# Delta rule on one core: doubling steps on 64 columns, sums of squares by a column of ones, and a new order between the dense products

## The chip, the core and the metric

The kernel runs on one core of a Trainium2 chip. Its engines are named as the profile names them: PE (TensorE matmul), PEld (its weight load), DVE (VectorE), ACT (ScalarE), POOL (GpSimd), SP (SyncE, which here issues the weight transfers). The metric is device time in microseconds (us); lower is better.

## The reference, cut to what matters

One decoder layer: a projection of 512 tokens by `w_in`, a gated delta rule over 8 heads, latent attention over 8 heads, an output projection and a gated feed-forward part. The change touches the delta rule of a head (and the order in which its steps stand between the products with `w_in`). With chunks of c = 64 tokens it is

```python
q = l2_normalize(q) * (dk ** -0.5)
k = l2_normalize(k)
gc = jnp.cumsum(g, axis=-1)
a_mat = jnp.where(strict, einsum("bhncd,bhnjd->bhncj", kb, k) * decay, 0.0)
sol = triangular_solve(a_mat + eye(c), concatenate([vb, kb * exp(gc)[..., None]]), lower=True)
u, w = sol[..., :dv], sol[..., dv:]
# then a scan over the chunks, with a state of 128 x 128
```

`l2_normalize` needs the sum of squares of each token's 128 channels. The triangular system is what the doubling steps solve. In the kernel a chunk is 128 tokens: NT = 4 tiles of P = 128.

## The kernel before

**Dense products.** All products with weights are made of two parts of float32r: `load_w` fetches a block of weights into `raw` (SP), ACT casts it to `whi` (L136), DVE makes the rest `wlo` (L137), and `mm3` (L143 to L145) issues three matmuls of 512 columns. One such block serves 24 matmuls. `raw` has two buffers, `whi` and `wlo` three, so a cast waits until PE is done with the block three before. Products collect in four PSUM banks `acc`.

**Delta rule.** `delta(h)` is a generator of three steps for a head. Step one transposes k (`transposed`, L466) to tokens on partitions, squares it on ACT with a running sum (L473, eight ACT instructions), takes the decays from one matmul (`gT`, L479), the products of k with k and q (`bank<-kq`), forms `bm`, and inverts the diagonal blocks of 16: `dd` (L511) goes out to DRAM and comes back replicated (`dr`, `rep`, L512 and L513, both issued by ACT's queue), and fifteen pairs of small DVE instructions (`xt`, `xs`, L519 and L521) end in `R` (L522). It also transposes v, and q only for its sum of squares (L547). Step two is `flip` (four transposes of R, L529, copied to `T` by ACT) and three doubling steps for b = 16, 32, 64: four matmuls of `bm` with `R`, a mask product on DVE (`Y`, L557), four matmuls of `T` with `Y`, and a subtraction on the odd blocks of R (L564); then the scan over the four tiles and the norm, which writes `on` in the buffer of `kbe` (L606). Step three transposes `on` (L611). These matmuls are plain float32: the trace has two PE instructions for each, and one for each transpose. They use four PSUM banks `bank`, shared by everything in `delta`.

**Order.** A string sets the order in which the steps of the heads of a pair (0 and 1) and of the dense products (p, a half of a part, 48 matmuls) are written down: `ORDER` for the first three pairs of heads, `LAST` for the fourth. The tile framework's list scheduler then places each instruction, in that order of priority, where its own planned times say it is ready, engine by engine. On the chip each engine works its list strictly in order. Heads 0, 2, 4, 6 are the even heads (the first of a pair), 1, 3, 5, 7 the odd ones.

Of the kernel before, what the change touches and what calls it, by code (L numbers as in the profile page):

```python
# [17 lines left out]
P = 128  # L18
# [15 lines left out]
# steps of a pair of heads of the delta rule (0, 1) between steps of the dense products (p)  # L34
ORDER = "0pp0p1pppp01p1"
LAST = "0pp0pp011pppppp1"
# [3 lines left out]
NEG = -1.0e30  # L40

C_UP, C_ONE, C_CAUS = (i * P for i in range(3))
C_LV = 3 * P
C_FREQ = C_LV + len(LEVELS) * P
# [8 lines left out]
def _pieces():  # L53
    """2*pi as three parts of 9 bits and a remainder."""
    out, rest = [], TWO_PI
    for k in range(3):
        e = math.floor(math.log2(rest))
        q = 2.0 ** (e - 8)
        c = math.floor(rest / q) * q
        out.append(c)  # L60
        rest -= c
    out.append(float(np.float32(rest)))
    return out
# [5 lines left out]
def _constants():  # L69
# [7 lines left out]
    for i, b in enumerate(LEVELS):  # L77
        blk = r // b
        m = (blk[:, None] % 2 == 0) & (blk[None, :] == blk[:, None] + 1)
        c[:, C_LV + i * P:C_LV + (i + 1) * P] = m  # L80
# [8 lines left out]
def layer_kernel(ctx: ExitStack, tc: tile.TileContext, x, positions, w_in, a_log, dt_bias, w_uq, w_ukv,  # L89
# [8 lines left out]
    def banks(**tags):  # L98
        """The eight banks of PSUM, by use, from here on."""
# [16 lines left out]
    def load_w(src, k, n, dst=None):  # L116
        """[P, k, n] of a weight as two float32r parts whose sum it is."""
# [45 lines left out]
    def over_tiles(ap):  # L163
        return ap.rearrange("p (o c) -> p o c", o=1).broadcast_to([P, NT, P])

    def rsq(out_ap, in_ap):
        """in ** -0.5"""
# [66 lines left out]
    def rows_of(pl_, col, dst, tag, bufs=1):  # L234
        """A scale per token, over tokens on the free side."""
# [39 lines left out]
    def split(dst_h, dst_l, src, w=None):  # L275
        """src (times a weight per partition) as two float32r parts."""
# [8 lines left out]
    def rotate(src, his, los, t1, t2):  # L285
        """Rotary of [2 x 64, tokens], each half in two parts."""
# [8 lines left out]
    def row(name, bufs=2):  # L295
        """Scratch of [P, S] in the slots of the delta rule."""
        return gd.tile([P, S], F32, name="s_" + name, tag=name, bufs=bufs)

# [34 lines left out]
    def gates():  # L333
# [9 lines left out]
        # log(1 + e) = 2 atanh(s), s = e / (2 + e) <= 1/3  # L343
# [32 lines left out]
    def rotary_tables():  # L376
        """cos and sin, frequencies on partitions."""
# [25 lines left out]
    heads = {}  # L403

    def project(hp, pre=()):
        """q, k, v (convolved, silu) and silu(z) of two heads, channels on partitions, in eight steps."""
# [43 lines left out]
    def delta(h):  # L450
        """A head of the delta rule, in three steps."""
# [17 lines left out]
        # decays between the tokens of a chunk  # L469
        ssk, rk, rk2, s1, s2, s3, ssq = (small(n) for n in ("ssk", "rk", "rk2", "s1", "s2", "s3", "ssq"))  # L470
        ktm = transposed(kT)
        for t4 in range(NT):
            nc.scalar.activation(junk, ktm[:, t4, :], AF.Square, accum_out=ssk[:, t4:t4 + 1])  # L473
        nc.vector.tensor_scalar(out=ssk, in0=ssk, scalar1=EPS, scalar2=None, op0=ALU.add)
# [11 lines left out]
        # B, of which what lies above the diagonal is never used, and the products of q and k  # L486
# [13 lines left out]
        # R = ((I + B)^-1)^T: blocks of 16 by substitution, a column of each block to a partition  # L500
        T, R, Y = sq("T", 1), sq("R"), sq("Y", 1)
# [30 lines left out]
        # k and v with tokens on partitions, scaled  # L532
# [12 lines left out]
        qtm = transposed(qT)  # L545
        for t4 in range(NT):
            nc.scalar.activation(junk, qtm[:, t4, :], AF.Square, accum_out=ssq[:, t4:t4 + 1])  # L547
# [3 lines left out]
        # and twice the size at each step  # L551
        flip(R, T)
        for i, b in enumerate(LEVELS):
            zp = bank()
            for t4 in range(NT):
                mm(zp[:, t4 * P:(t4 + 1) * P], bm[:, t4, :], R[:, t4, :])
            nc.vector.tensor_tensor(out=Y, in0=t4view(zp),  # L557
                                    in1=over_tiles(cst[:, C_LV + i * P:C_LV + (i + 1) * P]), op=ALU.mult)
            dp = bank()
            for t4 in range(NT):  # L560
                mm(dp[:, t4 * P:(t4 + 1) * P], T[:, t4, :], Y[:, t4, :])
            odd = R.rearrange("p t c -> p (t c)").rearrange("p (n w b) -> p n w b", w=2, b=b)[:, :, 1, :]
            dodd = dp.rearrange("p (n w b) -> p n w b", w=2, b=b)[:, :, 1, :]
            nc.vector.tensor_tensor(out=odd, in0=odd, in1=dodd, op=ALU.subtract)  # L564
# [3 lines left out]
        # -W^T, then the scan over the chunks  # L568
# [28 lines left out]
        # norm, gate  # L597
# [3 lines left out]
        nc.vector.tensor_scalar(out=ssq, in0=ssq, scalar1=EPS, scalar2=EPS * P, op0=ALU.add, op1=ALU.mult)  # L601
        nc.vector.scalar_tensor_tensor(out=sso, in0=sso, scalar=1.0 / P, in1=ssq, op0=ALU.mult, op1=ALU.add)
        rsq(f, sso)
        on = sq("kbe", 1)
# [10 lines left out]
    def latent(c0, accs):  # L615
        """A latent before its norm, channels on partitions, in four steps."""
# [15 lines left out]
    def normed(accs, w4, h_, l_, direct):  # L632
        """A latent, normalised, in two parts."""
# [32 lines left out]
    def dense():  # L666
        """The products with w_in, a step at a time."""
# [12 lines left out]
    # for the even head of a pair [low; high] parts, for the odd head [high; low]  # L680
# [315 lines left out]
```

## Time and profile before

| | us |
|---|---|
| median of 3 runs | 2462.61 (2461.74 to 2462.67) |
| span of the profiled execution | 2460.5 |
| PE busy in it | 2398.0 (97%) |
| PEld busy | 1965.9 (80%) |
| DVE busy | 1149.4 (47%) |
| ACT busy | 707.8 (29%) |

The span runs from the first to the last instruction; the runs' time is some 2 us longer. PE's busy time is a union of modelled matmul durations that overlap, so the distance from one start to the next, not the duration, is what a matmul costs in a row of them. The delta rule lies between 100 and 680 us of the span. In front of it and behind it PE works on products with weights.

### The profile page before, as it was taken

To read this page: it belongs to the slowest core of one execution; us is meant where nothing else is said; L and a number is where in the kernel's file an instruction comes from. 1 tells how busy PE (TensorE), PEld (TensorE's weight loads), DVE (VectorE), ACT (ScalarE), POOL (GpSimd) and SP (SyncE) were. 2 spreads that over 40 slices of the span, in tenths; PEclk is the share of its full clock that TensorE was granted. 3 is DMA by queue.
4 is the path that set the end of the run, shared out by engine and by line. 5 is a ranking of instruction groups with operands and counts; after the bars stand their busy time and mean duration, and the time that the engine had idled before them with its cause. 6 is when DMAs were issued, how large, how long until landed. Compare 5 with 4: busy or idle time off the path is not lost.

```text
span 2460.5 us, 27597 instructions
## 1 busy us (share of the span) xinstructions
PE 2398.0 (97%) x11142; PEld 1965.9 (80%) x11142; DVE 1149.4 (47%) x1850; ACT 707.8 (29%) x1154; POOL 80.1 (3%) x89
## 2 busy tenths in 40 slices
PE   8989999999999999999999999999999999999998
PEld 6777787777777778888888888888888888888886
DVE  6656565655555555433434333333334343434245
ACT  5332323333233333422222222222222222222223
POOL 0010101010000000000000000000000000000000
PEclk9999999999999999999999999999999999999999
DMA  5313232222422322333233333233333333332333
GB/s 177 79 52 78 69 87 62 85 69 70 133 69 65 90 65 67 106 95 102 86 103 97 101 94 99 89 103 94 104 94 95 102 95 95 102 95 87 107 98 111
DMA packets 199663, 225.87 MB, mean 92 GB/s; under 512 B 17264, under 2 KB 161776, under 8 KB 199408
## 3 DMA queue, kind: packets, MB, share of 16 engines
q1 hardware_dynamic: 194608, 214.15, 28.9%
q10 hardware_dynamic: 4928, 9.97, 1.3%
q8 instruction: 87, 1.43, 0.2%
q14 instruction: 40, 0.33, 0.0%
HBM read 219.63 MB, written 4.46 MB: 91 GB/s over the span
## 4 chain that ended last, share of the span: by engine, by line
PE 79%; DVE 3%; DMA 2%; ACT 2%; issue 1%; POOL 1%; ACTq 0%; POOLq 0%; DVEq 0%
PE acc L143 18%; PE acc L144 18%; PE acc L145 18%; PE bank L144 6%; PE bank L145 6%; PE bank L143 6%; PE bank L148 2%; PE score L148 1%; DMA rep<-dr 1%; DMA raw<-in_w_down 1%; PE op L148 1%; DVE wlo L137 1%; DVE t L290 0%; ACT whi L136 0%; PE bank L799 0%
## 5 line engine op out<-in xcount | busy, mean ns | idle before, releaser
L137 DVE TENSOR_TENSOR wlo<-raw,whi 128x1024 fp32r<-128x1024 f32 x386 | 469.1, 1215 | 714.5 <-ACT whi L136 708.4
L136 ACT CAST whi<-raw 128x1024 fp32r<-128x1024 f32 x386 | 403.7, 1046 | 1230.6 <-PE acc L144 687.2
L144 PE MATMUL acc<-fl,whi 128*128 128x512 f32 x1408 | 547.8, 389 | 0.0
L145 PE MATMUL acc<-fh,wlo 128*128 128x512 f32 x1408 | 547.7, 389 | 0.0
L143 PE MATMUL acc<-fh,whi 128*128 128x512 f32 x1408 | 547.6, 389 | 0.0
L144 PEld LDWEIGHTS acc<-fl,whi 128*128 128x128 f32 x1408 | 264.3, 188 | 54.9
L145 PEld LDWEIGHTS acc<-fh,wlo 128*128 128x128 f32 x1408 | 264.3, 188 | 54.8
L143 PEld LDWEIGHTS acc<-fh,whi 128*128 128x128 f32 x1408 | 264.2, 188 | 54.8
L143 PE MATMUL acc<-hh,whi 128*128 128x512 f32 (+1 forms) x656 | 266.6, 406 | 1.7 <-ACT whi L136 1.7
L144 PE MATMUL acc<-hl,whi 128*128 128x512 f32 (+1 forms) x656 | 265.6, 405 | 0.0
L145 PE MATMUL acc<-hh,wlo 128*128 128x512 f32 (+1 forms) x656 | 264.9, 404 | 0.0
L143 PE MATMUL bank<-whi,ah 128*128 128x512 f32 x640 | 249.0, 389 | 0.0
L144 PE MATMUL bank<-wlo,ah 128*128 128x512 f32 x640 | 249.0, 389 | 0.0
L145 PE MATMUL bank<-whi,al 128*128 128x512 f32 x640 | 249.0, 389 | 0.0
L918 DVE SCALAR_TENSOR_TENSOR x<-bank,rstd,x 128x512 f32<-128x512 f32 x160 | 119.8, 750 | 151.6 <-PE bank L145 151.6
L143 PEld LDWEIGHTS acc<-hh,whi 128*128 128x128 f32 (+1 forms) x656 | 124.5, 190 | 28.0 <-ACT whi L136 2.1
L144 PEld LDWEIGHTS acc<-hl,whi 128*128 128x128 f32 (+1 forms) x656 | 124.9, 190 | 26.0
L145 PEld LDWEIGHTS acc<-hh,wlo 128*128 128x128 f32 (+1 forms) x656 | 124.4, 190 | 26.2 <-issue 0.2
L143 PEld LDWEIGHTS bank<-whi,ah 128*128 128x128 f32 x640 | 120.1, 188 | 25.0
L145 PEld LDWEIGHTS bank<-whi,al 128*128 128x128 f32 x640 | 120.1, 188 | 24.9
L144 PEld LDWEIGHTS bank<-wlo,ah 128*128 128x128 f32 x640 | 120.1, 188 | 24.9
L143 PE MATMUL acc<-whi,mgh 128*128 128x512 f32 x256 | 103.4, 404 | 2.8 <-ACT mgh L278 2.5
(282 smaller groups left out, 2258.9 us busy)
## 6 DMA issues: line engine op xcount, KB each, us to landing
raw<-in_w_gate SPq DMA_DIRECT2D x88, 512.0 KB, 3.6
raw<-in_w_up SPq DMA_DIRECT2D x88, 512.0 KB, 3.6
raw<-in_w_down SPq DMA_DIRECT2D x88, 512.0 KB, 3.8
raw<-in_w_in SPq DMA_DIRECT2D x80, 512.0 KB, 3.7
raw<-in_w_out SPq DMA_DIRECT2D x32, 512.0 KB, 4.0
rep<-dr ACTq DMA_DIRECT2D x8, 512.0 KB
x<-in_x ACTq DMA_DIRECT2D x4, 1024.0 KB, 8.3
raw<-in_w_ukv SPq DMA_DIRECT2D x32, 128.0 KB, 2.6
```

The lines of the kernel that those rows point to most:

```text
L136: nc.scalar.copy(hi[:, :k * n], raw[:, :k * n])
L137: nc.vector.tensor_tensor(out=lo[:, :k * n], in0=raw[:, :k * n], in1=hi[:, :k * n].bitcast(F32), op=ALU.subtract)
L143: nc.tensor.matmul(ps, lhsT=lh, rhs=rh, start=start, stop=False)
L144: nc.tensor.matmul(ps, lhsT=lh, rhs=rl, start=False, stop=False)
L145: nc.tensor.matmul(ps, lhsT=ll, rhs=rh, start=False, stop=stop)
L148: nc.tensor.matmul(ps, lhsT=l, rhs=r, start=start, stop=stop)
L918: nc.vector.scalar_tensor_tensor(out=x2[:, t4, cs], in0=a, scalar=rstd[:, t4:t4 + 1], in1=x2[:, t4, cs], op0=ALU.mult, op1=ALU.add)
```

## The change

Five edits in `delta`, and the two strings (6).

1. The sums of squares of k and q: ACT squares the whole [128 x 512] once into the buffer `T`, and four matmuls with one column of ones sum over the channels. The transposes of q and the sixteen ACT instructions with a running sum go.
2. The doubling steps multiply only the 64 columns of a tile that change (the odd blocks): the moving side of the eight matmuls of a step has 64 columns in place of 128, DVE's mask product and the masks have 256 columns in place of 512.
3. `T` is taken at the start of a head (one buffer, as before).
4. `on` is written into `es`, which has two buffers, in place of `kbe`, which has one.
5. `ssq` is scaled in one DVE instruction as it is read from PSUM.
6. `ORDER` and `LAST` put three p ahead of the second step of the even head, and take one p from behind.

Comments are left out of the new file, so its line numbers differ by some ten.

```diff
-ORDER = "0pp0p1pppp01p1"
-LAST = "0pp0pp011pppppp1"
+ORDER = "0ppp0p1ppp01p1"
+LAST = "0ppp0pp011ppppp1"
...
-        c[:, C_LV + i * P:C_LV + (i + 1) * P] = m
+        c[:, C_LV + i * HALF:C_LV + (i + 1) * HALF] = m[:, blk % 2 == 1]
...
+        T = sq("T", 1)
+
+        def squares(src):
+            s2_ = T.rearrange("p t c -> p (t c)")
+            nc.scalar.activation(s2_, src, AF.Square)
+            qp = bank()
+            for t4 in range(NT):
+                mm(qp[:, t4:t4 + 1], s2_[:, t4 * P:(t4 + 1) * P], ones[:, 0:1])
+            return qp[:, 0:NT]
+
+        nc.vector.tensor_scalar(out=ssk, in0=squares(kT), scalar1=EPS, scalar2=None, op0=ALU.add)
         ktm = transposed(kT)
-        for t4 in range(NT):
-            nc.scalar.activation(junk, ktm[:, t4, :], AF.Square, accum_out=ssk[:, t4:t4 + 1])
-        nc.vector.tensor_scalar(out=ssk, in0=ssk, scalar1=EPS, scalar2=None, op0=ALU.add)
...
-        qtm = transposed(qT)
-        for t4 in range(NT):
-            nc.scalar.activation(junk, qtm[:, t4, :], AF.Square, accum_out=ssq[:, t4:t4 + 1])
+        nc.vector.tensor_scalar(out=ssq, in0=squares(qT), scalar1=EPS, scalar2=EPS * P, op0=ALU.add, op1=ALU.mult)
...
         for i, b in enumerate(LEVELS):
+            odd = R.rearrange("p t (n w b) -> p t n w b", w=2, b=b)[:, :, :, 1, :]
             zp = bank()
             for t4 in range(NT):
-                mm(zp[:, t4 * P:(t4 + 1) * P], bm[:, t4, :], R[:, t4, :])
+                mm(zp[:, t4 * HALF:(t4 + 1) * HALF], bm[:, t4, :], odd[:, t4])
...
             for t4 in range(NT):
-                mm(dp[:, t4 * P:(t4 + 1) * P], T[:, t4, :], Y[:, t4, :])
+                hs = slice(t4 * HALF, (t4 + 1) * HALF)
+                mm(dp[:, hs], T[:, t4, :], yh[:, hs])
...
-        on = sq("kbe", 1)
+        on = es
```

What the new strings make of the lists is seen at three places. All three are of head 2; heads 4 and 6 read alike.

PE at the flip of head 2, before (`R_1919` is that head's R, `bm_1900` its B; `acc_2231` is the first product of the next pair of heads, here seven matmuls into its first block of weights, `whi_2234`):

```order
L145 MATMUL acc_2231<-hh_76,wlo_2235 128x512
L143 MATMUL acc_2231<-hh_76,whi_2234 128x512
L529 MATMUL bank_2118<-fst_68,R_1919 128x128 x4
L148 MATMUL bank_2124<-R_1919,bm_1900 128x128 x4
L144 MATMUL acc_2231<-hl_77,whi_2234 128x512
```

The same place in the changed kernel (`R_1917`, `bm_1899`; `acc_2116` and `acc_2117` are the same products as `acc_2231` and `acc_2232` before):

```order
L145 MATMUL acc_2117<-hl_77,whi_2149 128x512
L146 MATMUL acc_2117<-hh_76,wlo_2150 128x512
L539 MATMUL bank_2178<-fst_68,R_1917 128x128 x4
L149 MATMUL bank_2184<-R_1917,bm_1899 128x64 x4
L144 MATMUL acc_2116<-hh_76,whi_2288 128x512
```

The flip now stands behind two whole blocks of the next pair (`whi_2119` and `whi_2149`), 48 matmuls, and not behind seven. Between the end of the kq products and the flip there are now 135 product matmuls; there were 98 (and one between the kq products).

PE in step one of head 2, some products behind the transposes of v, before (`acc_1990` and `acc_1991` are z of this pair):

```order
L144 MATMUL acc_1991<-hl_77,whi_1993 128x512
L145 MATMUL acc_1991<-hh_76,wlo_1994 128x512
L466 MATMUL bank_1979<-fst_68,kq_1217 128x128 x4
L143 MATMUL acc_1990<-hh_76,whi_2023 128x512
L144 MATMUL acc_1990<-hl_77,whi_2023 128x512
```

And changed (`T_1881` holds the squares of q, `cst_67` the ones):

```order
L146 MATMUL acc_1987<-hh_76,wlo_1990 128x512
L144 MATMUL acc_1986<-hh_76,whi_2019 128x512
L149 MATMUL bank_1978<-cst_67,T_1881 128x1 x4
L145 MATMUL acc_1986<-hl_77,whi_2019 128x512
L146 MATMUL acc_1986<-hh_76,wlo_2020 128x512
```

Four matmuls of one column stand where four transposes stood. A second group of four stands ahead of the transposes of k, where nothing stood.

ACT around the issue of `dr` of head 2, before (`whi_2083` is the last block of z, `whi_2234` the first of the next pair):

```order
L444 ACTIVATE vt_1869<-y_1862 128x512
L136 CAST whi_2083<-raw_2082 128x1024
L547 ACTIVATE junk_1877,ssq_1884<-bank_1979 128x128 x4
L542 ACTIVATE kdec_1966<-bank_1885,sc_302 128x128 x2
L512 DMA dr_1922<-dd_1921 128x64
L542 ACTIVATE kdec_1966<-bank_1885,sc_302 128x128 x2
L513 DMA rep_1923<-dr_1922 128x1x1024
L136 CAST whi_2234<-raw_2233 128x1024
```

And changed (`whi_2079` is the last block of z, `whi_2119` and `whi_2149` the first two of the next pair):

```order
L445 ACTIVATE vt_1865<-y_1858 128x512
L493 ACT_TABLE_LOAD
L493 ACTIVATE es_1898<-es_1898 128x512
L552 ACTIVATE kdec_1964<-bank_1889,sc_302 128x128 x4
L137 CAST whi_2079<-raw_2078 128x1024
L137 CAST whi_2119<-raw_2118 128x1024
L522 DMA dr_1920<-dd_1919 128x64
L523 DMA rep_1921<-dr_1920 128x1x1024
L137 CAST whi_2149<-raw_2148 128x1024
```

The issue of `dr` now stands behind the cast of the next pair's first block, which stood behind it.

## Rows read from the trace of the kernel before

**Rows 1.** The page, busy time, share and count of each engine.

```profile
PE 2398.0 (97%) x11142; PEld 1965.9 (80%) x11142; DVE 1149.4 (47%) x1850; ACT 707.8 (29%) x1154; POOL 80.1 (3%) x89
```

**Rows 2.** Windows: stretch, us, busy and (count) by engine; clock, DMA share, GB/s.

```profile
100.00:680.00 580.00, 542.20 (x2745) 440.86 (x2744) 344.15 (x785) 197.11 (x423) 56.90 (x59) 0.98 0.28 78
1000.00:2400.00 1400.00, 1400.00 (x6197) 1159.53 (x6196) 522.84 (x565) 330.73 (x363) 1.01 (x1) 1.00 0.32 97
```

**Rows 3.** Waits of PE, 100 to 680 us: us in total, times, longest.

```profile
PE bank L529 <- DVE R L522: 18.6, 5, 4.9
PE bank L148 <- ACT kdec L542: 3.5, 1, 3.5
PE bank L466 <- DVE es L497: 3.4, 3, 1.5
...
PE bank L611 <- DVE kbe L606: 2.2, 3, 0.8
...
PE bank L466 <- DVE kbe L606: 1.5, 1, 1.5
```

**Rows 4.** Timeline: start us, us, instruction xcount, [idle before]. Waits before flip or doubling.

```profile
116.84 1.99 PE L148 MATMUL bank<-kq 128*128 128x256 f32 x8
144.56 1.09 PE L529 MATMUL bank<-fst,R 128*128 128x128 f32 x4 [4.87 <-DVE R L522]
217.08 2.05 PE L148 MATMUL bank<-Y,T 128*128 128x128 f32 x8 [3.45 <-ACT kdec L542]
243.03 1.13 PE L148 MATMUL bank<-kq 128*128 128x256 f32 x4
272.27 1.09 PE L529 MATMUL bank<-fst,R 128*128 128x128 f32 x4 [3.36 <-DVE R L522]
597.75 0.66 PE L529 MATMUL bank<-fst,R 128*128 128x128 f32 x4 [2.51 <-DVE R L522]
```

**Rows 5.** Windows, columns as in rows 2: from PE's restart to full clock.

```profile
217.08:220.31 3.23, 3.23 (x12) 2.83 (x13) 1.41 (x2) 0.00 (x0) 0.00 (x0) 0.50 0.64 195
272.27:278.34 6.07, 6.07 (x25) 5.68 (x26) 1.68 (x2) 0.59 (x1) 1.09 (x1) 0.50 0.29 86
403.76:408.04 4.28, 4.28 (x20) 3.89 (x21) 1.67 (x2) 0.59 (x1) 1.07 (x1) 0.60 0.42 123
534.31:537.76 3.45, 3.45 (x15) 3.25 (x16) 1.62 (x2) 0.59 (x1) 1.09 (x1) 0.51 0.34 92
597.76:602.60 4.84, 4.84 (x25) 4.47 (x26) 3.15 (x4) 2.26 (x3) 0.00 (x0) 0.65 0.01 3
```

**Rows 6.** Timeline of PE at full clock: a group of small matmuls, and what follows.

```profile
112.29 0.60 PE L148 MATMUL bank<-sc,cst 128*128 128x32 f32 x4 [1.71 <-DVE sc L354]
112.73 0.47 PE L144 MATMUL acc<-hl,whi 128*128 128x512 f32 x1
...
119.81 0.65 PE L466 MATMUL bank<-fst,vt 128*128 128x128 f32 x4 [0.51 <-ACT qe L485]
120.22 0.48 PE L145 MATMUL acc<-hh,wlo 128*128 128x512 f32 x1
...
152.75 1.13 PE L148 MATMUL bank<-Y,T 128*128 128x128 f32 x8
153.64 0.48 PE L143 MATMUL acc<-hh,whi 128*128 128x512 f32 x1
```

**Rows 7.** Groups by shape, 100 to 680 us: busy, mean ns, idle before.

```profile
L557 DVE TENSOR_TENSOR Y<-bank,cst 128x512 f32<-128x512 f32 x24 | 16.6, 691 | 34.5 <-PE bank L148 34.5
...
L564 DVE TENSOR_TENSOR R<-R,bank 128x256 f32<-128x256 f32 x24 | 10.1, 420 | 27.4 <-PE bank L148 27.4
```

**Rows 8.** Timeline of head 2: the inversion of the blocks on ACT and DVE.

```profile
252.91 0.32 ACTq L512 DMA_DIRECT2D dr<-dd  x1
...
255.93 1.05 ACT L136 CAST whi<-raw 128x1024 fp32r<-128x1024 f32 x1 [2.03 <-PE acc L144]
...
271.07 1.05 DVE L522 TENSOR_TENSOR R<-xs,cst 128x512 f32<-128x512 f32 x1
```

## Prediction of the time after the change

> **What bounds the kernel now.** I read the page's busy times first: PE is busy for 97% of the span, no other engine for half of it [rows 1]. Behind 1000 us PE never stops and issues a matmul every 1400 / 6197 = 0.226 us [rows 2]; the change does not reach there. In the delta rule's stretch, 100 to 680 us, PE is busy for 542.2 of 580 us at a mean clock of 0.98 [rows 2]: it is still the engine that sets the end, but 38 us of it are waits. So an edit counts in two ways only: by what it adds to or takes from PE's own list, and by what it does to those waits. DVE (344 us) and ACT (197 us) have room in the stretch, and matter as links of a chain that PE waits for.
>
> The waits of PE come next [rows 3]. Five waits at the flip, for R, make 18.6 us. They are those of head 0 (4.87), head 2 (3.36), head 7 (2.51) [rows 4] and, by subtraction, 7.9 us of heads 4 and 6 together. One wait of 3.45 us stands in the first doubling step of head 1: its matmuls of T with Y need a bank that ACT's `kdec` frees, `kdec` of that head comes behind `kbe`, and `kbe` is written only when the `on` of head 0, in the same buffer, has been transposed. The rest, 3.4 + 2.2 + 1.5 us, are short waits where a head begins [rows 3]. Behind each of the long waits PE's granted clock is at its lower level, 1.2 GHz (0.50 of full), until it is back at 2.4 GHz [rows 5]. A stretch of length w at mean clock m, in which PE never waits, costs (1 - m) x w: 3.23 x 0.50 + 6.07 x 0.50 + 4.28 x 0.40 + 3.45 x 0.49 = 1.6 + 3.0 + 1.7 + 1.7 = 8.0 us for heads 1, 2, 4 and 6.
>
> **The order: what it takes from the waits.** In head 2 the chain from the kq products to R runs from 243.03 [rows 4] to 271.07 + 1.05 = 272.12 us [rows 8], 29.1 us. PE had work for 25.9 us of that. With 135 in place of 99 product matmuls between, it has 36 x 0.226 = 8.1 us more, and 0.5 us by the squares (below): 34.5 us. But the chain grows too. `dr` is issued at 252.91; in the new list of ACT it stands behind a cast that before began at 255.93, when PE was done with an older block, and took 1.05 us [rows 8]. That makes 257.0, and 0.5 us more since PE comes 0.5 us later to that point: the chain is 4.6 us longer, 33.7 us. PE arrives 0.8 us behind R, so the waits of heads 2, 4 and 6 go: 3.36 + 7.9 = 11.3 us, with the half clock behind them. What is late next is the flip itself, by 0.8 us only; the second rival is about that.
>
> The odd heads lose products there (139 or 140 in place of 171 in heads 3 and 5) and still have 139 x 0.226 + some 3.5 us of small matmuls = 34.9 us against the 29.1 us of head 2's chain, the nearest row. No wait comes there. Head 0 has 92 in place of 82 products: 2.3 us, and 0.5 us of squares; against that I set 0.5 us, since its `rep` is now issued behind a silu of z on ACT. Its wait shrinks by 2.3 us, from 4.87 to 2.6; that is near the 2.51 us of head 7, which had half clock behind it too [rows 4, 5], so I take nothing off for the clock. Head 7 has 93 in place of 94 products: no change.
>
> **`on` in `es`** frees `kbe` of the next head at once: `kbe` and `kdec` of an odd head no longer wait for the transposes of `on`. The 3.45 us of head 1 go, with 1.6 us of clock (in the 8.0).
>
> **The 64 columns: nothing on PE.** A doubling step has 16 PE instructions. A group of eight with 128 moving columns takes 153.64 - 152.75 = 0.89 us, 0.111 each; a group of four with 32 moving columns takes 112.73 - 112.29 = 0.44 us, 0.110 each [rows 6]. Both load 128 columns of weights for every instruction. A float32 matmul with fewer moving columns is thus no cheaper, whatever holds it at 0.11 us; 64 lies between 32 and 128, and I price it at 0.111. The bounds are 0.055 (half, which is the first rival) and 0.111. On DVE the mask product falls from 0.69 to about 0.42 us, that of the 256 columns beside it [rows 7], 24 times: 6.5 us. PE covers it with product matmuls, four of 0.226 before and three in the new list: 0.90 - 0.69 = 0.21 us to spare before, 0.68 - 0.42 = 0.26 now. So nothing comes of it on PE; without that cover it would be up to 6.5 us either way.
>
> **The column of ones: a loss on PE.** Four matmuls are eight PE instructions, 8 x 0.111 = 0.89 us by the same two rows, also with one moving column. A head has two such groups and loses one group of four transposes, 120.22 - 119.81 = 0.41 us [rows 6]: 1.78 - 0.41 = 1.37 us a head, 11.0 us for eight. The bounds are 0 (one column free, less 3.3 us of transposes: a gain) and 11.0. Of ACT sixteen instructions and their reads go, two of some 0.6 us come; ACT is not what PE waits for there. The new group at the head's front waits for a square of k in `T`, which is free once the head before has done its last doubling step, long ago in PE's list. The single scaling of `ssq` is one DVE instruction of four columns less: nothing.
>
> **Banks.** Each sum takes a fifth bank at the head's front, where four exist. PE waits in order, with the dense products behind it. The short waits there (7.1 us) can grow or go: between -7 and +8 us. I take 0, since the new list has five products between the decays and the kq products and eight behind the transposes of v, where banks are freed.
>
> **The sum**, on the profiled execution: 2460.5 - 11.3 (flips of heads 2, 4, 6) - 3.45 (head 1) - 8.0 (clock) - 2.3 (head 0) + 11.0 (squares) = 2446.5 us. The runs' median is 2.1 us above the span: 2448.6, say 2449.
>
> **Rival 1, columns count.** If a float32 matmul is paid by its moving columns, the doubling steps lose 24 x 16 x 0.055 = 21 us, and the squares cost nothing and save 3.3 us of transposes: 2462.6 - 25.0 - 21 - 3.3 = 2413. For it: eight instructions of 256 columns (the kq products) last 1.99 us, eight of 128 last 1.13 [rows 4, 6]. Against it: the row of 32 columns, which is one group only. The Trainium skill, "TensorE: Matmul & The Clock Gate", section "Back-to-back issue gap", tabulates the distance by moving columns alone, 134 cycles for 128 and about 60 for 64 or fewer, which would halve these matmuls. The row of 32 columns disagrees with that for float32 with a weight load each.
>
> **Rival 2, the flips still wait.** The margin of 0.8 us in heads 2, 4 and 6 rests on one cast and on DVE's order, where the reads of the z products stand among the small instructions of the inversion. If the chain is 4 us longer than I think, the three waits come back as they were: 11.3 us and 6.4 us of clock, 2449 + 17.7 = 2466, no change that can be told.
>
> **Rival 3, slower: the fifth bank.** The sum of squares of q needs a bank that in the odd heads only the products of `es` free, behind an exponential on ACT; in the even heads that exponential now stands behind a silu and one more table load. If PE must wait there, everything dense behind it waits too. It decides from where the waits exceed 14 us in all, 1.75 us in each of eight heads; the longest such wait so far is 1.5 us, three of them make 3.4 [rows 3]. At 2.5 us each, with 1.7 us of half clock behind, it is 8 x 4.2 = 34 us: 2449 + 34 = 2483.
>
> **How the numbers follow.** Forecast 0.72 (2441 to 2457), rival 1 0.06, rival 2 0.14 (partly come back: 2455 to 2467), rival 3 0.08. The range reaches from 2438 to 2462: it takes in the short waits' bounds and the half of rival 2, and leaves out rivals 1 and 3. What a measurement can tell from no change is 0.2%, 5 us: faster is below 2457.7, slower above 2467.5. Faster is the forecast, rival 1 and a little of rival 2: 0.80; same most of rival 2 and some of rival 3: 0.14; slower 0.06.
>
> **What would show it.** In the profile of the changed kernel: PE's count in the delta rule's stretch up by 8 x (16 - 4) = 96, and by some 11 us of start-to-start time; groups of 64 columns at 0.89 us to the next start, as those of 128; groups of one column the same. No wait at the flip in heads 1 to 6, one of 2 to 3 us in heads 0 and 7, no wait for `kdec`, and granted clock below 1.00 behind heads 0 and 7 alone. Wrong would be: groups of 64 columns at half the time (rival 1), waits for R in heads 2, 4 and 6 with `rep` issued late (rival 2), or new waits at the matmuls of one column or the transposes of v (rival 3).

## The result and the profile after

| | before | changed |
|---|---|---|
| median of 4 runs, us | 2462.64 (2461.74 to 2464.68) | 2436.18 (2435.13 to 2440.96) |
| span of the profiled execution, us | 2460.5 | 2434.6 |
| first score matmul of the attention, us | 690.70 | 666.13 |

The ratio is 0.9896, with a 95% interval of 0.9884 to 0.9907: 26.4 us faster. The forecast was 2449 (13.6 us faster) with a range of 2438 to 2462. The sign was right, the size was half of what came, and the time lies 2 us below the range. Of the 25.9 us between the two spans, 24.6 lie in front of the first score matmul, as expected of a change in the delta rule. The other 1.3 us are about what a stretch at the lower clock near the end cost the kernel before (0.24 x 7.00 = 1.7 us, below), which this execution of the changed kernel did not have there.

The page of the changed kernel (as [rows 1]), its window of the delta rule (as the first of [rows 2]) and its waits of PE from 100 to 680 us (as [rows 3]):

```profile
PE 2396.4 (98%) x11238; PEld 1971.7 (81%) x11238; DVE 1137.7 (47%) x1850; ACT 704.0 (29%) x1049; POOL 79.9 (3%) x89
```

```profile
100.00:680.00 580.00, 565.08 (x2965) 466.37 (x2963) 347.94 (x808) 201.08 (x332) 59.26 (x60) 0.99 0.29 82
```

```profile
PE bank L539 <- DVE R L532: 5.4, 2, 3.5
PE acc L144 <- ACT mgh L279: 2.5, 1, 2.5
PE bank L623 <- DVE es L618: 2.3, 3, 0.8
PE bank L149 <- DVE sc L355: 1.7, 1, 1.7
```

PE has 96 instructions more, and is busy for 565.1 of the 580 us, where it was for 542.2. The waits for `R` fell from five of 18.6 us [rows 3] to two of 5.4; the wait for `kdec` is gone; and so are all short waits of the transposes at a head's front (L466 before, 3.4 + 1.5 us in [rows 3] and two of 0.6 and 0.5 that are not shown there, 6.0 in all). Of the 7.1 us that the prediction called short waits, the 2.2 us of the transposes of `on` stay (2.3 now); 4.9 us went, and 1.1 us that it had not listed. What is left by name is the two flips, the transposes of `on`, and waits that have to do with other parts.

The timeline of PE at the places of [rows 4]: the flips of heads 0, 2 and 7.

```profile
145.85 0.63 PE L539 MATMUL bank<-fst,R 128*128 128x128 f32 x4 [1.85 <-DVE R L532]
234.72 1.89 PE L149 MATMUL bank<-kq 128*128 128x256 f32 x8
269.14 0.60 PE L539 MATMUL bank<-fst,R 128*128 128x128 f32 x4
582.77 1.08 PE L539 MATMUL bank<-fst,R 128*128 128x128 f32 x4 [3.53 <-DVE R L532]
```

The flip of head 2 stands without a wait in brackets; those of heads 4 and 6 too (only two waits are left in the sum above). In head 4 it is close: R is ready 0.17 us ahead of the flip, and flips that do wait start 0.15 us behind R. Head 0 waits 1.85 us where it waited 4.87, head 7 3.53 where it waited 2.51.

Prices on PE, from one start to the next as in [rows 6]: eight instructions of one column, and eight of 64 columns, each with the row behind.

```profile
122.73 0.95 PE L149 MATMUL bank<-cst,T 128*128 128x1 f32 x8
123.54 0.48 PE L146 MATMUL acc<-hh,wlo 128*128 128x512 f32 x1
...
149.59 0.60 PE L539 MATMUL bank<-fst,R 128*128 128x128 f32 x4
150.03 1.00 PE L149 MATMUL bank<-R,bm 128*128 128x64 f32 x8
150.84 0.47 PE L146 MATMUL acc<-hh,wlo 128*128 128x512 f32 x1
...
151.38 0.40 PE L145 MATMUL acc<-hl,whi 128*128 128x512 f32 x1
151.64 1.08 PE L149 MATMUL bank<-Y,T 128*128 128x64 f32 x8
152.53 0.47 PE L146 MATMUL acc<-hh,wlo 128*128 128x512 f32 x1
...
153.31 0.60 PE L539 MATMUL bank<-fst,R 128*128 128x128 f32 x4
```

One column: 0.81 us for eight. 64 columns: 0.81 and 0.89 us for eight, and 0.89 is what 128 columns took in [rows 6]. So fewer moving columns than 128 buy nothing here; what all these instructions share is a load of 128 columns of weights. That the load is what holds them is not shown: no run has a load of fewer columns. The Trainium skill, "TensorE: Matmul & The Clock Gate", section "LDWEIGHTS (loading the stationary operand)", gives a weight load as its columns over 1.2, in ns: that makes an estimate of 107 ns for 128 columns, and the trace's 0.10 to 0.11 us agree with it; the table by moving columns that the prediction weighed does not hold for these matmuls.

The clock, by windows as in [rows 5]. First the changed kernel: behind the wait for `sc` in front of head 0, behind the flip of head 0, behind that of head 7, and behind the wait for `mgh`:

```profile
114.85:118.26 3.41, 3.41 (x11) 2.83 (x10) 3.21 (x9) 1.00 (x3) 1.03 (x1) 0.50 0.16 31
145.85:152.00 6.15, 6.15 (x45) 5.30 (x45) 2.25 (x4) 1.17 (x2) 1.08 (x1) 1.00 0.30 85
582.77:590.00 7.23, 7.23 (x32) 6.65 (x32) 1.95 (x3) 1.63 (x2) 0.00 (x0) 0.55 0.00 0
637.22:642.70 5.48, 5.48 (x20) 3.92 (x20) 3.41 (x7) 2.00 (x4) 0.64 (x1) 0.70 1.05 383
```

and the kernel before at three of the same places (flip of head 0, `sc`, `mgh`), and near its end:

```profile
144.56:150.00 5.44, 5.44 (x26) 5.07 (x27) 0.84 (x2) 1.59 (x2) 0.15 (x1) 0.63 0.07 23
112.29:118.00 5.71, 5.68 (x29) 4.35 (x30) 2.78 (x9) 3.12 (x13) 1.03 (x1) 1.00 0.24 61
662.16:667.00 4.84, 3.77 (x18) 2.71 (x19) 3.41 (x7) 2.00 (x4) 0.00 (x1) 1.00 1.04 377
2415.00:2422.00 7.00, 6.89 (x24) 5.05 (x23) 4.89 (x9) 2.00 (x5) 0.55 (x1) 0.76 0.00 0
```

The half clock behind heads 1, 2, 4, 6 and 0 is gone, but two stretches at 1.2 GHz came behind waits of 1.7 and 2.5 us that had full clock behind them before. In all (1 - m) x w is 8.0 [rows 5] + 2.0 + 1.7 (heads 0 and 7) = 11.7 us before, and 1.7 + 3.3 + 1.6 = 6.6 us after.

### The profile page after: what moved, and what is told of

The parts are those of the page before. It is cut to its first block, busy times and chain, and to the rows that moved or that the text cites. A ratio compares the mean times of both kernels' runs of the same rounds, so it can differ in the third digit from the quotient of the medians.

```text
span 2434.6 us, 27687 instructions
## 1 busy us (share of the span) xinstructions
PE 2396.4 (98%) x11238; PEld 1971.7 (81%) x11238; DVE 1137.7 (47%) x1850; ACT 704.0 (29%) x1049; POOL 79.9 (3%) x89
## 3 DMA queue, kind: packets, MB, share of 16 engines
q1 hardware_dynamic: 194608, 214.05, 29.2%
## 4 chain that ended last, share of the span: by engine, by line
PE 92%; DVE 3%; DMA 2%; ACT 1%; issue 1%; POOL 1%; ACTq 0%; SPq 0%; POOLq 0%
PE acc L144 22%; PE acc L145 22%; PE acc L146 22%; PE bank L145 6%; PE bank L146 6%; PE bank L144 6%; PE bank L149 5%; PE score L149 1%; DMA raw<-in_w_down 1%; PE op L149 1%; DVE wlo L138 1%; DMA rep<-dr 1%; ACT whi L137 0%; PE bank L539 0%; DVE t L291 0%
## 5 line engine op out<-in xcount | busy, mean ns | idle before, releaser
L144 PEld LDWEIGHTS acc<-hh,whi 128*128 128x128 f32 (+1 forms) x656 | 124.3, 189 | 29.2 <-ACT whi L137 2.1
L145 PEld LDWEIGHTS acc<-hl,whi 128*128 128x128 f32 (+1 forms) x656 | 124.3, 189 | 26.6 <-issue 0.7
```

Of the source, the lines that this page charges most:

```text
L144: nc.tensor.matmul(ps, lhsT=lh, rhs=rh, start=start, stop=False)
L145: nc.tensor.matmul(ps, lhsT=lh, rhs=rl, start=False, stop=False)
```

## The experiments: one edit alone, and all but one

There are four edits that may stand alone: the strings, the squares, the columns, and `on` in `es`. Each was made alone on the kernel before, and each was taken back alone from the changed kernel. Ratios are to the kernel before on the same chip. "Waits for R" and "head fronts" (waits of the transposes of k, q and v and of the matmuls of one column) are sums from each profile, in us; "score" is the start of the first score matmul. The last three columns are of one execution each; that of all but `on` was the slowest of its four (2439.70), and lost 3.4 us more to the lower clock than that of the changed kernel (10.2 against 6.8, from 100 us to the first score matmul).

| kernel | median, us | ratio, 95% interval | waits for R | head fronts | score |
|---|---|---|---|---|---|
| strings alone | 2447.42 | 0.9939 (0.9922 to 0.9955) | 9.5 | 5.5 | 673.9 |
| squares alone | 2468.55 | 1.0020 (1.0011 to 1.0029) | 18.1 | 3.5 | 697.9 |
| columns alone | 2467.64 | 1.0014 (1.0005 to 1.0023) | 19.6 | 3.1 | 690.3 |
| `on` alone | 2461.10 | 0.9990 (0.9981 to 0.9999) | 18.3 | 6.0 | 690.5 |
| all but the strings | 2462.96 | 1.0006 (0.9997 to 1.0015) | 17.0 | 1.1 | 691.3 |
| all but the squares | 2437.95 | 0.9905 (0.9889 to 0.9922) | 7.8 | 2.4 | 668.0 |
| all but the columns | 2442.54 | 0.9924 (0.9910 to 0.9939) | 5.1 | 0.9 | 670.1 |
| all but `on` | 2435.83 | 0.9901 (0.9886 to 0.9916) | 5.4 | 0 | 669.0 |
| changed, again | 2438.71 | 0.9906 (0.9893 to 0.9920) | 5.5 | 0 | 666.8 |

**The strings alone.**

```diff
-ORDER = "0pp0p1pppp01p1"
-LAST = "0pp0pp011pppppp1"
+ORDER = "0ppp0p1ppp01p1"
+LAST = "0ppp0pp011ppppp1"
```

> The kernel before with the two new strings alone. Theory A (the order takes the waits at the flips of heads 2, 4 and 6, and nothing else): 11.3 us of waits and 6.4 us of half clock go, head 0's wait shrinks by about 1 us, head 1's wait for kdec (3.45 us and 1.6 us of clock) and the short waits at the heads' fronts (7.1 us) stay: 2462.6 - 18.7 = 2444 us. Rival B (the order also takes the short waits at the fronts, since the dense products of a half part more lie there): 2437 us, with no squares to pay for.

They gave 16.4 us (2463.86 to 2447.42), near theory A's 2444. The waits of PE in that profile:

```profile
PE bank L529 <- DVE R L522: 9.5, 4, 4.5
PE bank L466 <- DVE vb L544: 4.9, 3, 1.7
PE bank L148 <- DVE Y L557: 2.5, 4, 0.7
```

The even heads' waits are gone, and so is the one for `kdec`, which the prediction had put down to `on` in `es`. But the short waits stay, now as 4.9 us in front of the transposes of q in the odd heads, head 7 waits 4.5 us, and small waits for `Y` are new.

**The squares alone**.

```diff
...
+        T = sq("T", 1)
...
+        def squares(src):
+            s2_ = T.rearrange("p t c -> p (t c)")
+            nc.scalar.activation(s2_, src, AF.Square)
+            qp = bank()
+            for t4 in range(NT):
+                mm(qp[:, t4:t4 + 1], s2_[:, t4 * P:(t4 + 1) * P], ones[:, 0:1])
+            return qp[:, 0:NT]
...
-        qtm = transposed(qT)
-        for t4 in range(NT):
-            nc.scalar.activation(junk, qtm[:, t4, :], AF.Square, accum_out=ssq[:, t4:t4 + 1])
+        nc.vector.tensor_scalar(out=ssq, in0=squares(qT), scalar1=EPS, scalar2=EPS * P, op0=ALU.add, op1=ALU.mult)
```

> The kernel before with the sums of squares by a column of ones alone (old strings, 128 columns, on in kbe). The list then has 111 products in place of 98 between the kq products and the flip of heads 2, 4, 6. Theory A (the transposes of q held a bank until ACT had summed its squares, and that made the short waits at the fronts): PE pays 9.2 us more, the fronts' 6 us go, and 13 products and 0.5 us shorten each of the three flip waits by 3.4 us, so 10 us and most of their 6.4 us of clock go: 2462.6 + 9.2 - 6 - 10 - 5 = 2451 us. Rival B (the fronts' waits are not the transposes of q): 2457 us.

Both missed: it is slower by 4.7 us. In the old order the flips wait as before or longer (heads 2 and 4 in its timeline; head 4 waited 3.71 before):

```profile
271.37 1.08 PE L538 MATMUL bank<-fst,R 128*128 128x128 f32 x4 [4.05 <-DVE R L531]
...
408.95 1.08 PE L538 MATMUL bank<-fst,R 128*128 128x128 f32 x4 [5.38 <-DVE R L531]
```

So what the edit takes from the short waits does not pay for its matmuls, and the flips take no part of their price: R comes later too. From the start of the kq products to the end of R it takes 33.8 us in head 2 here, and 29.1 before.

**The columns alone** and **`on` alone**:

```diff
...
-                mm(zp[:, t4 * P:(t4 + 1) * P], bm[:, t4, :], R[:, t4, :])
+                mm(zp[:, t4 * HALF:(t4 + 1) * HALF], bm[:, t4, :], odd[:, t4])
...
-                mm(dp[:, t4 * P:(t4 + 1) * P], T[:, t4, :], Y[:, t4, :])
+                mm(dp[:, hs], T[:, t4, :], yh[:, hs])
...
```

> The kernel before with the doubling steps on 64 columns alone. Theory A (a float32 matmul with 64 moving columns costs 0.111 us like one with 128, DVE's shorter mask product is covered): 2462.6 us, within 3 us. Rival (the steps get shorter all the same, by DVE's 0.27 us in each of 24 steps): 2456 us.

```diff
-        on = sq("kbe", 1)
+        on = es
```

> The kernel before with on written into es alone. Theory A (only head 1's wait for kdec goes, 3.45 us and 1.6 us of clock; the other waits stay): 2457.5 us. Rival B (kbe, freed early, also takes the short waits at the fronts of the odd heads, some 5 us): 2452 us.

`on` alone gives 0.1%, at the edge of what can be told, and not the 5 us of its theory. The columns alone come out slower by 3.8 us, and the clock accounts for that: nine of their ten runs had a mean granted clock of 0.988 or 0.989, where the 25 runs of the kernel before had 0.991 to 0.994, and 0.003 of 2466 us is 7 us. (The profiled execution was the tenth, the fastest with 2460.95 and a clock of 0.992, so its rows are some 7 us better than the median.) The long wait of head 1 did not go with `on`: PE now waits at the same place for the next link of the chain, `Y`. The waits at the first doubling step of head 1, columns alone and `on` alone:

```profile
215.85 1.08 PE L149 MATMUL bank<-Y,T 128*128 128x64 f32 x8 [2.20 <-DVE Y L560]
```

```profile
216.99 1.13 PE L148 MATMUL bank<-Y,T 128*128 128x128 f32 x8 [1.84 <-DVE Y L557]
```

Added up, the four edits alone give -16.4 + 4.7 + 3.8 - 2.8 = -10.7 us. Together they give -26.4. Nearly half of the difference is clock. By the mean granted clock m of each run of length w (on record to 0.001), (1 - m) x w is on average 18.7 us before, 11.0 with the strings, 19.7 with the squares, 26.6 with the columns, 17.0 with `on`, and 11.0 in the changed kernel: -0.5 us for the single edits added up, -7.7 for all of them together. So about 7 of the 15.7 us are clock; that is an estimate, since it also counts what falls into waits. The next four runs look for the rest by taking one edit back from the changed kernel.

**All but the strings** (old `ORDER` and `LAST` in the changed kernel).

> The changed kernel with the old strings (squares by ones, 64 columns and on in es stay). Theory A, the three edits and the order lean on each other: with the old order the flips of heads 2, 4 and 6 wait again as in the run of the squares alone (4.05, 5.38 and 4.36 us, half clock behind each), and the 9.2 us of the squares' matmuls are paid: 2464 us. Rival B, the edits add up as they did one at a time (+4.7 squares, +3.8 columns, -2.8 on, on 2463.9): 2469.5. If the order is worth only what it gave alone (-16.4), it comes to 2452.6.

Theory A: 2462.96, no change against before (1.0006). The waits for R are back, 17.0 us in five. So the strings are worth 27 us where the other edits stand (by the two ratios, 1.0006 against 0.9896), and 16 alone; and the other edits are worth nothing without the strings. What they save on PE in the old order (the fronts and `kdec`) is about what the squares' matmuls cost, and the flips of heads 2, 4 and 6 go on waiting. The chains to R, further below, show why.

**All but the squares** (squares as before in the changed kernel).

> The changed kernel with the sums of squares as before (transposes of q, sixteen ACT instructions). Theory A, the squares' edit takes the waits at the front of the odd heads away because the transposes of q, which wait there for a bank that DVE reads, are gone: PE gets back 9.2 us of matmuls, and the waits of the run of the strings alone return (three of 1.65 us in front of the transposes of q, head 0 by 2 us, flips of odd heads and first products of Y by 3 us, head 7 by 1 us, each with some 0.17 us of restart): 2436.2 - 9.2 + 12 = 2439 us. Rival B, those waits go by another edit (on in es or the columns): 2427 to 2429 us.

Theory A, 2439 expected, 2437.95 measured. Its waits:

```profile
PE bank L530 <- DVE R L523: 7.8, 3, 3.9
...
PE bank L467 <- DVE es L498: 1.9, 3, 0.7
```

The waits in front of the transposes of q return, though smaller than with the strings alone, and the flips of heads 0 and 1 wait longer. The matmuls of one column cost about 10 us of PE, and are paid back in waits: with them or without them the time is the same within the intervals.

**All but the columns** (128 columns in the changed kernel).

> The changed kernel with the doubling steps on 128 columns, as before. Theory A, columns cost nothing on PE (0.112 us for 64 and 128) and DVE's longer mask product lies beside product matmuls: 2436 us, at most 2 off. Rival B, the shorter mask products (24 times 0.27 us) shorten the waits of PE between the matmuls of a step: 2442 us. Rival C, the 64 columns cost as they seemed to alone (+3.8): 2432 us.

Rival B: 2442.54, 6 us above the changed kernel (and 6.7 above the run without `on`, on the same chip; the four runs of one and of the other do not overlap). PE's price is the same; the difference is a wait too short for the sums of waits. This is the doubling step with 128 columns, from its timeline, which answers to the rows of 64 columns above:

```profile
148.24 0.64 PE L538 MATMUL bank<-fst,R 128*128 128x128 f32 x4
148.71 1.06 PE L148 MATMUL bank<-R,bm 128*128 128x128 f32 x8
...
150.30 0.39 PE L143 MATMUL acc<-hh,whi 128*128 128x512 f32 x1
150.64 1.13 PE L148 MATMUL bank<-Y,T 128*128 128x128 f32 x8
...
152.31 0.63 PE L538 MATMUL bank<-fst,R 128*128 128x128 f32 x4
```

From the last product to the matmul with `Y` it is 0.34 us here, and 151.64 - 151.38 = 0.26 with 64 columns, where a product takes 0.23. Both have their mask product on DVE beside the products:

```profile
L564 DVE TENSOR_TENSOR Y<-bank,cst 128x512 f32<-128x512 f32 x24 | 16.5, 689 | 30.0 <-PE bank L148 30.0
```

```profile
L568 DVE TENSOR_TENSOR Y<-bank,cst 128x256 f32<-128x256 f32 x24 | 10.1, 423 | 28.4 <-PE bank L149 28.4
```

From one flip to the next a step takes 152.31 - 148.24 = 4.07 us with seven products here, and 153.31 - 149.59 = 3.72 us with six in the changed kernel. Less the products at 0.2265 us each, that is 2.48 against 2.36: 0.12 us in each of 24 steps, 3 us. Three waits at heads' fronts add 0.9, one in head 1 adds 0.6, and four more waits cost some 0.16 us more each than their rows say (the account of the prediction has why): 5.1 us. By the start of the first score matmul the two profiled executions are 4.0 us apart; this one lost 1.7 us less to the lower clock on the way (5.1 against 6.8). Without that it is 5.7 us, near the 6 us between the medians.

**All but `on`** (`on` in `kbe` in the changed kernel).

> The changed kernel with on in kbe, as before. Theory A, the prediction's step: on in es is what took head 1's wait for kdec away; it comes back with its half clock: 2436.2 + 3.5 + 1.6 = 2441 us. Rival B, the new order has taken that wait away by itself (the run of the strings alone shows no wait for kdec): 2436 us, no wait for kdec in the profile.

Rival B: 2435.83, no `kdec` among the waits. With the new order `on` in `es` does nothing that can be told.

## The experiments: which half of the squares, and a faster kernel

These four ran on one chip, the changed kernel among them (2438.71, the table's last row).

**Squares of k as before, those of q by ones.**

```diff
-        nc.vector.tensor_scalar(out=ssk, in0=squares(kT), scalar1=EPS, scalar2=None, op0=ALU.add)
         ktm = transposed(kT)
+        for t4 in range(NT):
+            nc.scalar.activation(junk, ktm[:, t4, :], AF.Square, accum_out=ssk[:, t4:t4 + 1])
+        nc.vector.tensor_scalar(out=ssk, in0=ssk, scalar1=EPS, scalar2=None, op0=ALU.add)
```

> The changed kernel with the squares of k as before (ACT, from the transposed k) and those of q by the column of ones. Theory A, the two halves of the edit do different things: the matmuls for k (64 PE instructions, 64 x 0.099 = 6.4 us) buy a shorter chain to R, those for q take the transposes of q out of the odd heads' front. So PE gains 6.4 us and loses what the flips' waits of heads 0, 1 and 7 were longer with all squares as before (3.27, 0.54, 3.95 against 1.85, 0, 3.53 us, with 0.5 us of restart and clock); no wait at a transpose of q: 2436.2 - 6.4 + 3.0 = 2433 us. Rival B, the waits of R do not come back: 2430. Rival C, what is gained on PE is lost again wholly: 2436.

All three missed: 2442.69, slower by 4.0 us than the changed kernel (their runs overlap by 0.4 us, 2441.68 to 2443.61 against 2436.73 to 2442.08), with 64 PE instructions fewer. Its waits:

```profile
PE bank L541 <- DVE R L534: 9.4, 5, 3.3
...
PE bank L149 <- DVE es L509: 1.9, 3, 0.7
```

Heads 1, 3 and 5 wait for R now, and the matmuls of one column of q wait where the transposes of q did. The head-3 flip of the changed kernel shows why that was near: R is ready at 327.82 + 1.08 = 328.90, and PE comes at 330.87.

```profile
327.82 1.08 DVE L532 TENSOR_TENSOR R<-xs,cst 128x512 f32<-128x512 f32 x1
...
330.87 0.60 PE L539 MATMUL bank<-fst,R 128*128 128x128 f32 x4
```

So it is the squares of k that keep the chain to R short in the odd heads, and not the missing transposes of q that clear the head's front. The waits that came (3.9 us for R, 2.4 at the fronts) are about the 6.4 us saved. The 4 us more are in the two traces too: 0.9 us of waits of the kq products, 11 waits more, each some 0.16 us longer than its row (1.8 us), and 1.7 us more lost to the lower clock up to the first score matmul (8.5 against 6.8).

The even heads go the other way, and there the traces show how the edits lean on each other. Two times decide at each flip: when R is ready, and when PE comes to the flip. Both are counted here from the start of the head's kq products, in us, from the timelines; head 2 stands for the even heads 2, 4 and 6, head 3 for the odd heads 3 and 5.

| kernel | head 2: R ready | PE comes | head 3: R ready | PE comes |
|---|---|---|---|---|
| before | 29.1 | 29.2 (waits) | 31.2 | 49.9 |
| strings alone | 29.6 | 35.2 | 39.4 | 39.5 (waits) |
| squares alone | 33.8 | 33.9 (waits) | 33.9 | 48.1 |
| all but the strings | 32.5 | 32.7 (waits) | 33.4 | 45.7 |
| all but the squares | 29.6 | 35.3 | 37.5 | 38.1 |
| squares of k as before | 32.4 | 35.7 | 39.6 | 39.6 (waits) |
| changed | 33.6 | 34.4 | 33.8 | 35.8 |

With the strings alone PE comes 6 us later to the even heads' flips and 10 us earlier to the odd ones, where R also comes 8 us later (what holds it there stays open). That leaves 5.6 us to spare in the even heads and none in the odd ones. There a shorter chain counts, and the other edits shorten it: the columns and `on` from 39.4 to 37.5 us, the squares to 33.8. In the old order R has 12 us and more to spare in head 3, so the same edits gain nothing there. The squares also make R 4 us later in the even heads (29.1 to 33.8 with the old strings, 29.6 to 33.6 with the new): in the old order the flips wait for that, in the new one it falls into the room that the strings made. Of k alone, with the new strings, R is 1.2 us later in head 2 and 5.8 earlier in head 3.

These are the rows of `dr` and R of head 2, with the strings alone (its kq products start at 236.99):

```profile
246.89 0.32 ACTq L512 DMA_DIRECT2D dr<-dd  x1
...
265.49 1.08 DVE L522 TENSOR_TENSOR R<-xs,cst 128x512 f32<-128x512 f32 x1
```

and with the squares alone (from 237.46):

```profile
250.97 0.32 ACTq L521 DMA_DIRECT2D dr<-dd  x1
...
270.17 1.05 DVE L531 TENSOR_TENSOR R<-xs,cst 128x512 f32<-128x512 f32 x1
```

The new place of `dr` on ACT, behind two casts, was shown ahead of the prediction as the work of the new strings, and the prediction priced it there. It is the squares': with the strings alone `dr` goes out 9.9 us behind the kq products and ahead of the second cast, as before; with the squares alone it goes out after 13.5 us, behind two casts, as in the changed kernel. This is read from the traces and not tested by itself: each edit makes the scheduler write all lists anew, and no run changes an edit and keeps the lists, so what a run shows is the edit with its lists.

**Squares and ones in float32r**, two columns of ones:

```diff
+    onr = const.tile([P, 2], F32R, name="onr")
+    nc.vector.tensor_copy(onr, ones[:, 0:2])
...
-        T = sq("T", 1)
+        s2_ = gd.tile([P, S], F32R, name="sqr", tag="T", bufs=1)
...
-                mm(qp[:, t4:t4 + 1], s2_[:, t4 * P:(t4 + 1) * P], ones[:, 0:1])
-            return qp[:, 0:NT]
+                mm(qp[:, 2 * t4:2 * t4 + 2], s2_[:, t4 * P:(t4 + 1) * P], onr[:, 0:2])
+            return qp[:, 0:2 * NT:2]
...
+        T = sq("T", 1)
         flip(R, T)
```

> The changed kernel with the squares and the ones in float32r (two columns of ones), one PE instruction for each matmul where float32 has two. Theory A, PE is paid by instructions: 64 fewer at 0.099 us, 6.4 us less, 2430 us, with groups of four at some 0.4 us. Rival B, a float32r matmul of 128 weight columns costs 0.2 us as a whole, however many columns move: 2436 us.

Theory A: 2432.02 (2430.01 to 2434.99), 0.9879 of before (0.9865 to 0.9892), 6.7 us under the changed kernel on its chip, where 6.4 were expected; their runs do not overlap. The page has 64 PE instructions fewer (11174 against 11238), and a group of four goes by in 121.62 - 121.20 = 0.42 us:

```profile
121.20 0.56 PE L149 MATMUL bank<-onr,sqr 128*128 128x2 f32 x4
121.62 0.48 PE L146 MATMUL acc<-hh,wlo 128*128 128x512 f32 x1
```

This is the fastest kernel of the study. Its waits for R are 5.1 us, against 5.5 in the changed kernel on that chip: here, where PE is behind R by then, a microsecond saved on PE is a microsecond of the time. In head 2 nothing is left of that: R is ready 0.15 us ahead of the flip, which is the distance of flips that wait.

**Squares of k as before, those of q by ones in float32r** (the two edits above together).

> Squares of k as before, those of q by ones in float32r. By theory A of both runs before this one 3.2 us under the run with k as before: 2430 us. By rival B of float32r as that run: 2433 us. If both theories fall: 2436.

2439.35: 3.3 us under the first of these runs. The price of 32 instructions says 3.2, but its odd heads still wait for R (9.6 us in five), and up to the first score matmul the profiled execution lost 3.4 us less to the lower clock than that of the first (5.1 against 8.5); so the agreement shows little. It missed its 2430, as the first run, its start, had missed by 10 us.

**The changed kernel again.**

> The changed kernel unaltered, on the chip of these three, to compare them with: 2436 us, at most 2 off.

2438.71 (2436.73 to 2442.08), 0.7 above the upper end that I gave.

## Why the prediction was off, step by step

The terms, as predicted and as the rows above show them (us; the squares by rows: 16 groups at 0.81, less eight groups of transposes at 0.41 [rows 6]). The measured ones add up to -25.7, against 25.9 between the spans:

| term | predicted | measured |
|---|---|---|
| waits for R, heads 2, 4, 6 | -11.3 | -11.3 |
| wait for R, head 0 | -2.3 | -3.0 |
| wait for R, head 7 | 0 | +1.0 |
| `kdec` of head 1 | -3.45 | -3.5 |
| half clock | -8.0 | -5.1 |
| squares on PE | +11.0 | +9.7 |
| short waits at heads' fronts | 0 (-7 to +8) | -6.0 |
| 64 columns, time from flip to flip less the products | 0 | about -3 |
| behind the delta rule | 0 | -1.3 |
| 13 waits fewer, at 0.16 us above their rows | not in the sum | -2.1 |
| a wait for `ssl` behind the delta rule | not in the sum | -1.1 |

- **The step that failed is the banks**: "I take 0". All 6.0 us of short waits went, near the low end of my own bounds. I had looked at the products that stand around the new groups, but not at what frees a bank: DVE's reads, above all those behind `es`. In head 3 DVE's last product of `es` ends 7.0 us behind the start of the kq products; where the squares of k are taken back, alone or with those of q, it ends after 10.3 and 10.4, and the three waits of heads 1, 3 and 5 behind `es` are back, at some 0.6 us each. The runs: 6.0 us before, 5.5 with the strings alone, 3.5 with the squares alone, 3.1 with the columns alone, 1.1 with all but the strings, 2.4 with all but the squares, 0.9 with all but the columns, 0 in the changed kernel. No edit does it alone, and a sum over edits taken one at a time had no place for it. How the 6.0 us divide among the edits stays open.
- **The 64 columns at zero** were right on PE (0.81 to 0.89 us for eight, whatever the columns) and wrong beside it. I set four products of 0.226 against a mask product of 0.69 and called the rest spare; but from PE's last matmul to DVE and back to PE some 0.3 us pass as well, so that PE waited 0.11 us in front of `Y`, too short for the sums of waits. With 64 columns and three products it waits 0.03. With the rest of the step that is 0.12 us a step, 3 us; taking the columns back costs 6 us in all.
- **The waits for R** are right as a sum, and head 2 as predicted to 0.1 us: from 234.72 to 267.26 + 1.06 = 268.32 the chain takes 33.6 us (33.7 predicted), and PE comes at 269.14, 0.8 us behind R. That is luck. I had the chain grow by 4.6 us because the new order puts a cast ahead of `dr`; but the order alone leaves the chain at 29.6 us, and it is the squares that lengthen it. The timeline of that head on ACT and DVE, as [rows 8]:

```profile
241.57 0.63 ACT L493 ACTIVATE es<-es 128x512 f32<-128x512 f32 x1
242.24 0.87 DVE L505 SCALAR_TENSOR_TENSOR bm<-bank,s,es 128x128 f32<-128x128 f32 x3 [0.51 <-ACT es L493]
...
246.79 1.05 ACT L137 CAST whi<-raw 128x1024 fp32r<-128x1024 f32 x1 [2.61 <-PE acc L145]
246.92 1.04 DVE L521 TENSOR_REDUCE dd<-Y 128x64 f32<-128x512 f32 x1
248.00 0.32 ACTq L522 DMA_DIRECT2D dr<-dd  x1
251.12 0.60 ACTq L523 DMA_DIRECT2D rep<-dr  x1
...
267.26 1.06 DVE L532 TENSOR_TENSOR R<-xs,cst 128x512 f32<-128x512 f32 x1
```

  The cast ended at 247.84, as I had said it would hold `dr`; but `dd` was ready only at 247.96, since `bm` had waited for the exponential of `es`, which now stands behind a silu and a table load on ACT. I had named that delay in rival 3 and not in the chain. So `dr` was issued 13.3 us behind the kq products, 3.4 later than before and not 4.6. `rep`, which needs `dr` to have landed, followed after 3.1 us; before it was 1.55 (254.46 - 252.91). From 248.00 to 251.12 the DMA engines were busy for 0.88 of the time, from 252.91 to 254.46 before for 0.10: a fetch of weights, issued at 247.02, now runs beside `dr`. The rest was 0.5 us shorter. 3.4 + 1.6 - 0.5 gives 4.5 us, by other terms than mine.
- **The odd heads** do not wait for R, as predicted, but not with the 5.8 us to spare that I had (34.9 against 29.1): it is 35.8 against 33.8 in head 3. Head 2's chain was the wrong row for them. With the strings alone theirs takes 39.4 us; the columns and `on` bring it to 37.5, the squares to 33.8.
- **The wait for `kdec`** went, but not by `on` in `es`: the strings alone take it away, and putting `on` back into `kbe` in the changed kernel brings no wait for `kdec`. Right size, wrong cause.
- **Head 7** was to stay and grew by 1.0 us, with 93 in place of 94 products to cover a chain that I had not looked at.
- **The half clock**: what I expected to go went, and head 0's 2.0 us too; but 3.3 us came behind waits for `sc` and `mgh`, which cost nothing in clock before, and head 7's grew from 1.7 to 3.3.
- **Not in the sum**: each wait costs 0.16 us more than its row says. Between two products it is 0.23 us from start to start, while a wait is counted from the modelled end, 0.39 us behind the start. From 100 us to the first score matmul PE has 25 waits over 0.1 us before and 12 after: 13 x 0.16 = 2.1 us. And a wait of 1.07 us for `ssl`, at 665.4 us before, has no counterpart after; why is not shown.

Rival 1 (columns count) fell by the rows of 64 and of one column. Rival 2 (the flips still wait) did not come, but only just: the margin is 0.8 us in heads 2 and 6 and 0.17 us in head 4, hardly more than the 0.15 of a flip that waits. Rival 3 (the fifth bank) did not come: no matmul of one column has a wait in the changed kernel, though with the squares alone the longest is 1.4 us.

## What to carry to other kernels

Where an engine waits at several places, edits do not add. For each wait note two times, when the chain is ready and when the engine comes, and ask of every edit what it does to both, at every place: the squares moved some 4 us of chain from the odd heads to the even ones, where the strings had made room. Work taken off the engine is worth all of it where the engine comes later than its chains (the float32r squares, 6.7 of 6.4 expected), for as long as it does. Price the removal of the long waits first, and then ask of every short wait in the same stretch which links of its chain each edit takes away. A DVE step that PE covers with products needs a cover longer than the step itself, here by the 0.3 us of passing from engine to engine. And compare the granted clock of the runs before a few us between two kernels are put down to what an edit does on an engine.

## What the hardware showed

- A float32 matmul cost 0.10 to 0.11 us for each of its two PE instructions at 1, 64 and 128 moving columns, and a float32r matmul of two columns 0.10 us in one instruction.
- Waits of the same length at the same place are followed by the lower clock in one kernel and by the full clock in the other: 1.7 us in front of `sc` (1.00 before, 0.50 after), 2.5 us for `mgh` (1.00 before, 0.70 after). Which waits will cost clock could not be read from their length.
- Runs of one kernel differ by their granted clock: the four of the changed kernel took 2435.13, 2435.89, 2436.46 and 2440.96 us at 0.997, 0.996, 0.996 and 0.993.
- The small transfer `dr` took 1.55 us from issue to the next link with the DMA engines busy for 0.10 of the time, and 3.1 us with 0.88.
